# One decoder layer on one core: the turn on which FFN-down takes its fourth pair of half buffers

## The chip, the cores and the metric

The kernel runs on one core of a Trainium2 chip. The metric is the device time of one execution, in microseconds (us); the time of a kernel is the median of several executions. TensorE (PE) multiplies, VectorE (DVE) and ScalarE (ACT) work element by element, GpSimd (POOL) and SyncE (SP) are used here almost only to issue transfers (DMAs) from HBM.

## The reference

One layer of a decoder for 256 tokens of width 2048, all in float32. Cut to the part around the change:

```python
h2 = rms_norm(x, mlp_norm[i])
x = x + jnp.square(jax.nn.relu(h2 @ w_ffn_up[i])) @ w_ffn_down[i]
gate = jax.nn.sigmoid(rms_norm(x, ple_norm[i]) @ w_ple_gate[i])
x = x + gate * (p[i] @ w_ple_proj[i])
return rms_norm(x, final_norm)
```

Ahead of it stand a pooling mixer, an RWKV-7 time mixer and their output product, which the change does not touch. `w_ffn_up` is 2048 x 8192 and `w_ffn_down` 8192 x 2048, 64 MB each; with 256 tokens they are most of the work and most of the bytes.

## The kernel before, in words

**Halves.** Every product is made in TensorE's fast float32 form from two halves of each operand: a high half (what the fast form keeps of the number) and a low half (the rest). A weight block therefore goes through the same steps everywhere: SP loads it raw from HBM (`load_raw`, L158, tiles `raw_*`), ACT copies it in one or two pieces of 128x512 into the high half `wh_*` (L167 in the general helper, L172 in `split_sb`, L1278 in FFN-down), DVE subtracts it from the raw block to get the low half `wl_*` (L168, L173, L1279), and PE multiplies with both.

**Half buffers.** A pair of half buffers (one for `wh`, one for `wl`, 128x1024 each) is free again when PE has made the last product with it. There are three such pairs in the pool `wp` (tags `wh`, `wl`), used in rotation by all stages, and one further pair in the pool `fp` (tags `wh4`, `wl4`) that only FFN-down uses.

**FFN-up.** `ffn_half(hf)` runs twice, each time for one half of the 8192 columns. Its first part makes eight column blocks f (`gemm_wide`, L1112 and L1117; bank `u_w`), each in two halves of four weight blocks `u`. The three pairs in `wp` rotate: weight block k is split into the pair that block k-3 has left. PE needs about the time of four groups of two `wh` and two `wl` products for one weight block. After each half block come the squared ReLU and its halves (`square`: L1356 on ACT, L1357 and L1358 on DVE, tile `r`, then `y`), for seven-product squares also sums of activations (`activation_sums`, tiles `s`, `S`).

**FFN-down.** Its second part is two `down_sweep`s, (hf, pair) for pair 0 and 1, each over 16 square blocks kp of four 512-wide quarters. A square outside `SEVEN` costs eight products of quarters: raw blocks `raw_d_<kp>_0` and `raw_d_<kp>_1`, split into the pairs `<kp>a` and `<kp>b`. A square in `SEVEN` = 1, 3, 4, 6, 8, 9, 11, 13 costs seven (Winograd's form) and needs sums of weight quarters. One of these sums is made by DMA: POOL issues a plain load (L1232) and, when it has landed, a load that adds (L1233) into one of two slots of the tile `ring`. The square's second pair `<kp>b` holds the halves of one raw quarter and, beside it, the halves of this sum from the ring (two ACT copies at L172, two DVE subtractions at L173). From the sum DVE makes `t2` in place (L1313), then two more differences in place in the raw block (L1315); the halves of `t2` go to the tile `wa`, those of the raw block to the pair `<kp>d`, which in three of the four sweeps has buffers of its own. The operands of PE's products stand at L1262 (high by high), L1263 (with the low half of the weight) and L1264 (with the low half of the activation).

**The ring.** `begin_sum` begins the next sum in the list. The first two are begun in FFN-up of the first half, after column blocks 4 and 5 (L1231 is a one-element copy that ties it to `r`); each further one after a seven-product square, into the slot which that square has done with.

**The turn.** `half_tiles` (L1266 to L1271) hands out the pairs of FFN-down. A list `turns`, kept over all four sweeps, counts the calls; on every fourth the pair comes from `fp`, on the other three from `wp`. A sweep takes 32 turns, the last one 37. In a first sweep the order of turns begins 0a, 0b, 1a, 1b, 2a, 2b, 3a, 3b.

**The order.** From FFN-up on, the order of the instructions on each engine is set by the framework's scheduler, which places each instruction by priority as soon as its operands and its buffer are free in its own model of time. The splits of weights and what belongs to them have a raised priority (`tc.high_priority(20000)`). Each engine then runs its list strictly in order: an instruction that waits holds up all that stand behind it on that engine.

Of the kernel before, what the change touches and what calls it, by code (L numbers as in the profile page):

```python
# [40 lines left out]
def trunk(  # L41
# [1176 lines left out]
    turns = []  # L1218
# [20 lines left out]
    def down_sweep(hf, pair, ys, sboxes, hooks=(), between=None):  # L1239
# [26 lines left out]
        def half_tiles(name):  # L1266

            turns.append(name)
            if len(turns) % 4 == 0:
                return [fp.tile([128, 1024], F32R, tag=f"{hl}4", name=f"{hl}_{name}") for hl in ("wh", "wl")]  # L1270
            return [wp.tile([128, 1024], F32R, tag=hl, name=f"{hl}_{name}") for hl in ("wh", "wl")]  # L1271

        def halves_of(src, name, own=False):

            wh, wl = [fp.tile([128, 1024], F32R, tag="graw", bufs=2, name=f"{hl}_{name}") for hl in ("wh", "wl")] if own and hf + pair < 2 else half_tiles(name)
            with tc.high_priority(20000):
                for c in range(2):
                    nc.scalar.activation(wh[:, c * 512 : c * 512 + 512], src[:, c * 512 : c * 512 + 512], AF.Copy)  # L1278
                nc.vector.tensor_tensor(wl, src, wh.bitcast(F32), op=ALU.subtract)  # L1279
            return [(wh[:, c * 512 : c * 512 + 512], wl[:, c * 512 : c * 512 + 512]) for c in range(2)]  # L1280
# [12 lines left out]
        for q, kp in enumerate(visits):  # L1293
# [5 lines left out]
            if kp in seven:  # L1299
                i = SEVEN.index(kp)  # L1300
                st = sboxes[kp][:, i % 2 * 1024 : i % 2 * 1024 + 1024]
                s1, s2_, s3, s4 = ((st[:, c * 128 : c * 128 + 128], st[:, 512 + c * 128 : 640 + c * 128]) for c in range(4))
                p1 = summed(hf, pair, kp)
                t2 = p1
                wa = fp.tile([128, 1024], F32R, tag="junk", bufs=1, name=f"wa{nm}_{kp}")
                w2 = wa[:, 0:512], wa[:, 512:1024]
                w21, w11 = halves_of(rx, f"{nm}_{kp}a")
                wh, wl = half_tiles(f"{nm}_{kp}b")
                w22, w1 = ((wh[:, c : c + 512], wl[:, c : c + 512]) for c in (0, 512))
                with tc.high_priority(20000):  # L1310
                    split_sb(*w22, ry[:, 0:512])
                    split_sb(*w1, p1)
                    nc.vector.tensor_tensor(t2, p1, ry[:, 0:512], op=ALU.subtract)  # L1313
                    t43 = rx.rearrange("p (r n) -> p r n", r=2)
                    nc.vector.tensor_tensor(t43, t43, t2.unsqueeze(1).to_broadcast([128, 2, 512]), op=ALU.subtract)  # L1315
                    split_sb(*w2, t2)
                w4, w3 = halves_of(rx, f"{nm}_{kp}d", True)
                for n, a_, w_ in (("1", a11, w11), ("2", a12, w21), ("3", s4, w22), ("5", s1, w1), ("6", s2_, w2), ("4", a22, w4), ("7", s3, w3)):
                    prod(n, a_, w_)
                begin_sum()  # L1320
            else:
                w21, w11 = halves_of(rx, f"{nm}_{kp}a")
                for n, a_, w_ in (("2", a12, w21), ("4", a22, w21), ("2", a11, w11), ("4", a21, w11)):
                    prod(n, a_, w_)
                w22, w12 = halves_of(ry, f"{nm}_{kp}b")
                for n, a_, w_ in (("3", a12, w22), ("x", a22, w22), ("3", a11, w12), ("x", a21, w12)):
                    prod(n, a_, w_)
# [209 lines left out]
```

## Time and profile before

| | |
|---|---|
| three timed runs | 1179.17, 1180.53, 1183.03 us; median 1180.53 |
| the profiled execution | 1182.91 us, of which 1181.1 us from its first to its last instruction (span) |
| FFN-up, first half | about 378 to 563 us of the span |
| its two sweeps | 563 to 727 us |
| FFN-up and two sweeps, second half | 727 to 1072 us |
| DVE, ACT busy over the span | 877.7 us (74%), 714.1 us (60%) |
| mean granted clock of TensorE | 0.995 of full speed |

All times in the trace are in us from the start of the span. A timeline row gives start, duration, engine, line, operation, tiles, shape, number of instructions merged and, in square brackets, how long the engine had been idle and what released it. PE's instructions overlap: two that start 0.23 us apart last 0.39 us each, so that PE's pace is read from starts and not from durations. A tile's name has its numbers left out: `u_w` is the bank of any column block, and `wh_d_1b` that of square 1 in any of the four sweeps.

### The profile page before, as it was taken

To read this page: it belongs to the slowest core of one execution; us is meant where nothing else is said; L and a number is where in the kernel's file an instruction comes from. 1 tells how busy PE (TensorE), PEld (TensorE's weight loads), DVE (VectorE), ACT (ScalarE), POOL (GpSimd) and SP (SyncE) were. 2 spreads that over 40 slices of the span, in tenths; PEclk is the share of its full clock that TensorE was granted. 3 is DMA by queue.
4 is the path that set the end of the run, shared out by engine and by line. 5 is a ranking of instruction groups with operands and counts; after the bars stand their busy time and mean duration, and the time that the engine had idled before them with its cause. 6 is when DMAs were issued, how large, how long until landed. Compare 5 with 4: busy or idle time off the path is not lost.

```text
span 1181.1 us, 17409 instructions
## 1 busy us (share of the span) xinstructions
PE 1162.8 (98%) x6407; PEld 973.1 (82%) x6407; DVE 877.7 (74%) x1194; ACT 714.1 (60%) x1323; POOL 58.5 (5%) x133
## 2 busy tenths in 40 slices
PE   9999999999999999999999999999999999999997
PEld 8787777788887888878888888888888888888886
DVE  8686996954656676757888988676768988897543
ACT  8777858676545565545665664555556665677543
POOL 2100000000000000000110110000000110000000
PEclk9999999999999999989999999999999999999999
DMA  8454443354454555555687686555555886975511
GB/s 294 154 199 144 142 143 109 119 179 161 175 190 171 179 190 191 198 171 204 202 241 244 200 245 233 194 182 194 186 189 174 248 250 228 316 247 190 198 56 72
DMA packets 67253, 224.42 MB, mean 190 GB/s; under 512 B 7712, under 2 KB 8480, under 8 KB 66784
## 3 DMA queue, kind: packets, MB, share of 16 engines
q1 hardware_dynamic: 60240, 207.38, 50.2%
q0 software_dynamic: 6496, 15.21, 5.7%
q8 instruction: 50, 0.82, 0.3%
q10 hardware_dynamic: 432, 0.73, 0.2%
q14 instruction: 35, 0.29, 0.1%
HBM read 221.19 MB, written 2.10 MB: 189 GB/s over the span
## 4 chain that ended last, share of the span: by engine, by line
PE 93%; DVE 3%; DMA 2%; ACT 2%; issue 1%; POOL 0%; SPq 0%; DVEq 0%; POOLq 0%; ACTq 0%
PE u_w L1112 19%; PE u_w L1117 10%; PE d_b L1262 7%; PE d_b L1264 7%; PE d_b L1263 7%; PE d_w L1262 2%; PE d_w L1264 2%; PE d_w L1263 2%; PE gt_b L238 2%; PE gt_b L241 2%; PE gt_b L242 2%; PE o_b L241 1%; PE o_b L242 1%; PE zv_b L238 1%; PE o_b L238 1%; PE zp_b L238 1%
## 5 line engine op out<-in xcount | busy, mean ns | idle before, releaser
L1112 PE MATMUL u_w<-h,wh_u 128*128 128x512 f32 x1024 | 323.8, 398 | 1.8 <-ACT wh_u L167 1.8
L167 ACT ACTIVATE wh_u<-raw_u 128x512 fp32r<-128x512 f32 x256 | 147.4, 623 | 154.9 <-issue 95.5
L168 DVE TENSOR_TENSOR wl_u<-raw_u,wh_u 128x1024 fp32r<-128x1024 f32 x128 | 156.7, 1224 | 104.6 <-ACT wh_u L167 102.9
L1117 PEld LDWEIGHTS u_w<-h,wl_u 128*128 128x128 f32 x1024 | 193.6, 189 | 47.2 <-DVE wl_u L168 1.5
L1117 PE MATMUL u_w<-h,wl_u 128*128 128x256 f32 x1024 | 202.6, 279 | 0.9 <-DVE wl_u L168 0.9
L1112 PEld LDWEIGHTS u_w<-h,wh_u 128*128 128x128 f32 x1024 | 157.0, 190 | 2.0 <-ACT wh_u L167 2.0
L168 DVE TENSOR_TENSOR wl_gt<-raw_gt,wh_gt 128x1024 fp32r<-128x1024 f32 x24 | 29.4, 1224 | 23.2 <-ACT wh_gt L167 23.1
L172 ACT ACTIVATE wad<-ring 128x512 fp32r<-128x512 f32 x29 | 18.2, 629 | 43.1 <-DVE ring L1313 43.1
L167 ACT ACTIVATE wh_gt<-raw_gt 128x512 fp32r<-128x512 f32 x48 | 28.0, 639 | 23.0 <-PE gt_b L242 14.4
L241 PE MATMUL gt_b<-wh_gt,h 128*128 128x512 f32 x96 | 37.3, 389 | 0.0
L242 PE MATMUL gt_b<-wh_gt,h 128*128 128x512 f32 x96 | 37.3, 389 | 0.0
L1315 DVE TENSOR_TENSOR raw_d<-raw_d,ring 128x1024 f32<-128x1024 f32 x29 | 35.5, 1222 | 0.7
L1232 POOL DMA_DIRECT2D ring<-in_w_ffn_down_dram x29 | 16.5, 570 | 356.8 <-DVE r L1358 190.8
L1233 POOL DMA_DIRECT2D ring<-in_w_ffn_down_dram x29 | 25.4, 876 | 110.4 <-DMA ring<-in_w_ffn_down_dram 110.4
L168 DVE TENSOR_TENSOR wl_o<-raw_o,wh_o 128x1024 fp32r<-128x1024 f32 x16 | 19.6, 1223 | 12.9 <-ACT wh_o L167 11.4
L167 ACT ACTIVATE wh_o<-raw_o 128x512 fp32r<-128x512 f32 x32 | 18.4, 623 | 16.3 <-issue 8.5
L167 ACT ACTIVATE wh_zp<-raw_zp 128x512 fp32r<-128x512 f32 x32 | 18.6, 624 | 15.8 <-PE zp_b L242 7.1
L168 DVE TENSOR_TENSOR wl_zk<-raw_zk,wh_zk 128x1024 fp32r<-128x1024 f32 x16 | 19.4, 1220 | 9.8 <-ACT wh_zk L167 9.8
L241 PE MATMUL zv_b<-wh_zv,hTh 128*128 128x512 f32 x64 | 26.0, 406 | 0.0
L241 PE MATMUL zk_b<-wh_zk,hTh 128*128 128x512 f32 x64 | 25.2, 394 | 0.6 <-ACT wh_zk L167 0.6
L241 PE MATMUL zp_b<-wh_zp,hTh 128*128 128x512 f32 x64 | 25.7, 401 | 0.0
L238 PE MATMUL gt_b<-wl_gt,h 128*128 128x512 f32 x96 | 25.7, 389 | 0.0
(927 smaller groups left out, 3007.2 us busy)
## 6 DMA issues: line engine op xcount, KB each, us to landing
raw_u<-in_w_ffn_up_dram SPq DMA_DIRECT2D x128, 512.0 KB, 3.5
raw_d<-in_w_ffn_down_dram SPq DMA_DIRECT2D x99, 512.0 KB, 4.7
ring<-in_w_ffn_down_dram POOLq DMA_DIRECT2D x58, 256.0 KB, 4.5
raw_gt<-in_w_ple_gate_dram SPq DMA_DIRECT2D x24, 512.0 KB, 3.5
raw_zk<-in_w_in_dram SPq DMA_DIRECT2D x16, 512.0 KB, 3.7
raw_zr<-in_w_in_dram SPq DMA_DIRECT2D x16, 512.0 KB, 3.3
raw_zv<-in_w_in_dram SPq DMA_DIRECT2D x16, 512.0 KB, 3.3
raw_zp<-in_w_in_dram SPq DMA_DIRECT2D x16, 512.0 KB, 3.2
```

The costliest lines, as they stand in the source:

```text
L167: nc.scalar.activation(wh[:, a * 512 : (a + 1) * 512], raw[:, a * 512 : (a + 1) * 512], AF.Copy)
L168: nc.vector.tensor_tensor(wl, raw, wh.bitcast(F32), op=ALU.subtract)
L238: nc.tensor.matmul(banks[tt], ah[:, ts_], halves[a][1], start=False, stop=last)
L241: nc.tensor.matmul(banks[tt], ah[:, ts_], halves[a][0], start=i + a == 0, stop=False)
L242: nc.tensor.matmul(banks[tt], al[:, ts_], halves[a][0], start=False, stop=False)
L1112: nc.tensor.matmul(bank[:, ct, :].rearrange("p (s t) -> p s t", s=2), wh[:, cs[ct]], hl, start=k == 0, stop=False, skip_group_check=True,)
L1117: nc.tensor.matmul(bank[:, ct, 0:T], wl[:, cs[ct]], hl[:, 0, :], start=False, stop=k == 15, skip_group_check=True)
L1233: nc.gpsimd.dma_start(slot(n), w_down[pair, hf * 16 + kp, 0, :, 1, :], accum_op=ALU.add)
L1262: nc.tensor.matmul(banks[n], ah, wh, start=first, stop=False)
L1263: nc.tensor.matmul(banks[n], ah, wl, start=False, stop=False)
L1264: nc.tensor.matmul(banks[n], al, wh, start=False, stop=last)
L1315: nc.vector.tensor_tensor(t43, t43, t2.unsqueeze(1).to_broadcast([128, 2, 512]), op=ALU.subtract)
```

## The change

One number changes: the pair from `fp` is handed out on turns 1, 5, 9 and so on, and no longer on turns 4, 8, 12.

```diff
         def half_tiles(name):
 
             turns.append(name)
-            if len(turns) % 4 == 0:
+            if len(turns) % 4 == 1:
                 return [fp.tile([128, 1024], F32R, tag=f"{hl}4", name=f"{hl}_{name}") for hl in ("wh", "wl")]
             return [wp.tile([128, 1024], F32R, tag=hl, name=f"{hl}_{name}") for hl in ("wh", "wl")]
```

Before, a first sweep's 0a, 0b and 1a take the three pairs that FFN-up leaves, in the order in which it leaves them, and 1b takes the pair in `fp`. Now 0a takes the pair in `fp`, and 0b, 1a and 1b take those that FFN-up leaves. From 2a on every turn again takes the pair of the turn four before it, as it did. Where a second sweep ends and FFN-up follows, the last three turns now hold all three pairs of `wp`; before, it was the last four without the last. No instruction is added or taken away; the scheduler places some of them elsewhere. POOL's list stays as it was.

On ACT, in FFN-up of the first half, just behind the column block that begins the first sum of the ring (`S` is a sum of activations, `wh_u` FFN-up's high halves, `wh_d_1b` those of square 1's second pair):

```order
 L172 ACTIVATE S_4690<-s_4801 128x512
 L167 ACTIVATE wh_u_1_4934<-raw_u_1_4932 128x512 x2
-L172 ACTIVATE wh_d_1b<-ring 128x512
 L167 ACTIVATE wh_u_2_4957<-raw_u_2_4955 128x512 x2
 L1356 ACTIVATE r_0_4902<-u_w_4809 128x512
```

The copy of the ring's sum into the high half of 1b is gone from this place; DVE's list loses its low half (`wl_d_1b<-ring`) at the same place.

On ACT, at the last column block of FFN-up (block 7, its second half, whose weight blocks are `u_0` to `u_3`):

```order
 L172 ACTIVATE y_5018<-r_1_5211 128x512
 L167 ACTIVATE wh_u_0_5327<-raw_u_0_5325 128x512 x2
+L1278 ACTIVATE wh_d_0a<-raw_d_0_0_5429 128x512 x2
 L172 ACTIVATE S_5010<-s_5217 128x512
 L167 ACTIVATE wh_u_1_5350<-raw_u_1_5348 128x512 x2
 L167 ACTIVATE wh_u_2_5373<-raw_u_2_5371 128x512 x2
 L1356 ACTIVATE r_0_5318<-u_w_5225 128x512
-L172 ACTIVATE wh_d_1b<-raw_d_1_1_5469 128x512
 L167 ACTIVATE wh_u_3_5396<-raw_u_3_5394 128x512 x2
-L172 ACTIVATE wad_1_5471<-ring 128x512
-L1278 ACTIVATE wh_d_0a<-raw_d_0_0_5429 128x512 x2
 L172 ACTIVATE y_5224<-r_0_5318 128x512
```

The copies of 0a move ahead of three of FFN-up's last four blocks; the other half of 1b and the halves of `t2` (`wad`) leave FFN-up.

On DVE, where the first sweep begins (`r` is the last squared ReLU of FFN-up):

```order
 L1279 TENSOR_TENSOR wl_d_1a<-raw_d_1_0_5467,wh_d_1a 128x1024
+L173 TENSOR_TENSOR wl_d_1b<-raw_d_1_1_5469,wh_d_1b 128x512
+L173 TENSOR_TENSOR wl_d_1b<-ring,wh_d_1b 128x512
 L1357 TENSOR_TENSOR r_1_5417<-u_w_5324,r_1_5417 128x512
+L1313 TENSOR_TENSOR ring<-ring,raw_d_1_1_5469 128x512
+L1358 SCALAR_TENSOR_TENSOR r_1_5417<-r_1_5417 128x512
 L1315 TENSOR_TENSOR raw_d_1_0_5467<-raw_d_1_0_5467,ring 128x1024
-L1358 SCALAR_TENSOR_TENSOR r_1_5417<-r_1_5417 128x512
+L173 TENSOR_TENSOR wad_1_5471<-ring,wad_1_5471 128x512
 L1279 TENSOR_TENSOR wl_d_2a<-raw_d_2_0_5515,wh_d_2a 128x1024
 L1279 TENSOR_TENSOR wl_d_1d<-raw_d_1_0_5467,wh_d_1d 128x1024
```

Four operations of square 1 (both halves of 1b, `t2` at L1313 and its low half) now stand here, ahead of 1d; the last `y` of FFN-up, which stood between 2b and 3a, now stands behind 3b. The second half's first sweep is changed in the same two ways (its first sum is begun in the second sweep before it, so that its 1b stood early in FFN-up too). The SP list changes only in the order of a few raw loads of the first squares.

## The prediction

> **What bounds the kernel now.** I read the page first. PE is busy 98% of the span, and its granted clock is at the top in every slice but one:
>
> ```profile
> PE 1162.8 (98%) x6407; PEld 973.1 (82%) x6407; DVE 877.7 (74%) x1194; ACT 714.1 (60%) x1323; POOL 58.5 (5%) x133
> PEclk9999999999999999989999999999999999999999
> ```
>
> So a change that removes no product can gain only where PE stands or runs slowly. The 8 is the slice from 502 to 531 us, in FFN-up. The windows around it (PE's busy time and instructions first, granted clock and DMA last):
>
> ```profile
> core 0: us, PE busy (x) PEld busy (x) DVE busy (x) ACT busy (x) POOL busy (x), PEclk, DMA share, GB/s
> 499.00:509.00 10.00, 8.61 (x51) 7.34 (x49) 1.73 (x3) 1.99 (x4) 0.88 (x1) 1.00 0.55 153
> 509.00:519.00 10.00, 8.72 (x33) 7.11 (x34) 7.22 (x8) 5.33 (x11) 0.00 (x0) 0.66 0.44 158
> 519.00:529.00 10.00, 10.00 (x59) 8.71 (x58) 7.64 (x12) 5.99 (x11) 1.73 (x3) 1.00 0.60 206
> ```
>
> Where 59 products start in a normal stretch, 51 and 33 start here; PE idles for a while, and then it runs at 0.66 of its clock. The waits of 495 to 515 us say for whom:
>
> ```profile
> ACT wh_d_1b L172 <- DMA ring<-in_w_ffn_down_dram: 7.9, 1, 7.9
> ...
> PE u_w L1112 <- ACT wh_u L167: 1.8, 1, 1.8
> ...
> PE u_w L1117 <- DVE wl_u L168: 0.9, 1, 0.9
> ```
>
> PE waits for FFN-up's next halves; ACT, which makes them, has stood 7.9 us at a copy that FFN-down will want only some 60 us later: the ring's half of 1b, which could start so early because its buffer, the pair in `fp`, was free. The ring's sum was still on its way. The chain of waits gives its two transfers, the timeline the rest:
>
> ```profile
> 496.31 4.65 DMA ring<-in_w_ffn_down_dram
> ...
> 501.27 6.81 DMA ring<-in_w_ffn_down_dram
> ```
>
> ```profile
> 499.10 1.15 ACT L167 ACTIVATE wh_u<-raw_u 128x512 fp32r<-128x512 f32 x2 [1.11 <-issue]
> ...
> 506.05 0.63 PE L1112 MATMUL u_w<-h,wh_u 128*128 128x512 f32 x2
> 506.75 0.63 PE L1112 MATMUL u_w<-h,wh_u 128*128 128x512 f32 x2
> 508.17 0.63 ACT L172 ACTIVATE wh_d_1b<-ring 128x512 fp32r<-128x512 f32 x1 [7.91 <-DMA ring<-in_w_ffn_down_dram]
> 508.70 1.13 ACT L167 ACTIVATE wh_u<-raw_u 128x512 fp32r<-128x512 f32 x2
> 509.37 0.87 PE L1112 MATMUL u_w<-h,wh_u 128*128 128x512 f32 x2 [1.76 <-ACT wh_u L167]
> 511.74 1.05 PE L1112 MATMUL u_w<-h,wh_u 128*128 128x512 f32 x2
> 513.02 1.05 PE L1112 MATMUL u_w<-h,wh_u 128*128 128x512 f32 x2
> 516.77 0.63 PE L1112 MATMUL u_w<-h,wh_u 128*128 128x512 f32 x2
> ```
>
> PE's groups of two high and two low products start 0.70 us apart (506.05 to 506.75). The next was due at 507.45 and started at 509.37: 1.92 us lost. Up to 516.77 it starts five groups, which at 0.70 take 3.50, so the sixth was due at 507.45 + 3.50 = 510.95 and came at 516.77: **5.82 us lost** in all. After the second pause the groups are 1.28 us apart (511.74 to 513.02), nearly double, until the clock comes back. The lost time is therefore 1.92 and 0.91 us of waiting and 3.0 us of slow clock.
>
> **What the change does, part by part.**
>
> *It removes the early copy.* 1b no longer has a free buffer in FFN-up, so its copy leaves this place on ACT (and its low half on DVE) and comes back at the sweep's start, when that sum has been in the ring for 50 us. Nothing else in ACT's list at this place waits for a DMA of the ring: the next entry is `wh_u`, whose raw block SP loads ahead. Gain: 5.82 us, once. In the second half the same copy sat early too, but there its sum had been begun in the sweep before; PE shows no wait there, so it gains nothing.
>
> [...] The idle rows are 1.8 and 0.9 us, and the clock fell. [...]
>
> *It puts 0a early into FFN-up.* ACT now copies 0a (two pieces) behind the first of the last four weight blocks. What is queued behind it on ACT is FFN-up's next `wh_u`, for which PE waits. The raw block of 0a must have landed by then:
>
> ```profile
> raw_d<-in_w_ffn_down_dram SPq DMA_DIRECT2D x1, 512.0 KB, 3.5
> ```
>
> ```profile
> 543.57 0.33 SPq L158 DMA_DIRECT2D raw_d<-in_w_ffn_down_dram  x1
> ```
>
> ```profile
> 546.76 1.15 ACT L167 ACTIVATE wh_u<-raw_u 128x512 fp32r<-128x512 f32 x2 [1.16 <-issue]
> ```
>
> It lands at 543.57 + 3.5 = 547.1; ACT is through with the block ahead at 547.9. So there is no wait, with 0.8 us to spare, and if the load is late ACT has the slack of FFN-up besides: in the stall above the copy would have started at 501.9 (one block, 4 x 0.70, after 499.10), started at 508.70, and PE was 1.92 us late, so 4.9 us are free. Cost: none. ACT's 1.15 us and DVE's 1.22 us for 0a only change places. SP: raw loads of the first squares are issued in another order, each still behind a buffer that comes free no later than before; no cost.
>
> *It delays 1b at the start of both first sweeps.* 1b, `t2` and its halves now queue there. Rows of before, DVE, ACT, PE and POOL:
>
> ```profile
> 569.27 1.22 DVE L1279 TENSOR_TENSOR wl_d_1d<-raw_d,wh_d_1d 128x1024 fp32r<-128x1024 f32 x1
> ...
> 571.54 0.68 DVE L173 TENSOR_TENSOR y<-r,y 128x512 fp32r<-128x512 f32 x1
> ...
> 577.83 1.23 DVE L1279 TENSOR_TENSOR wl_d_3d<-raw_d,wh_d_3d 128x1024 fp32r<-128x1024 f32 x1 [0.68 <-ACT wh_d_3d L1278]
> ...
> 586.05 1.22 DVE L1279 TENSOR_TENSOR wl_d_4d<-raw_d,wh_d_4d 128x1024 fp32r<-128x1024 f32 x1
> ```
>
> ```profile
> 563.48 1.15 ACT L1278 ACTIVATE wh_d_1a<-raw_d 128x512 fp32r<-128x512 f32 x2 [1.64 <-issue]
> ...
> 579.89 0.62 ACT L172 ACTIVATE wh_d_4b<-ring 128x512 fp32r<-128x512 f32 x1
> ```
>
> ```profile
> 572.53 0.39 PE L1263 MATMUL d_b<-wl_d_1d,y 128*128 128x512 f32 x1
> ...
> 587.50 0.39 PE L1263 MATMUL d_b<-wl_d_4d,y 128*128 128x512 f32 x1
> ```
>
> 1a had waited for FFN-up's last pair until 563.48; now 1b gets that pair, then. From its first ACT copy on (0.63, till 564.1) DVE has, up to 1d: six small ones of 0.68 (1b twice, L1357, L1313, L1358, `wad`) and two large ones of 1.22 (L1315, 2a), 6.5 us by whole durations, so 1d starts at 570.6 and is ready at 571.8 where PE takes it at 572.53. That is 0.7 us to spare, or more, since the rows overlap a little. DVE is then at most 1.4 us behind the row of before (570.6 against 569.27). The `y` that moved behind 3b is passed on, and the gap of 0.68 before 3d is used up, which leaves 0 to 0.7 us at square 4. There the rows are tightest: `wl_d_4d` ends at 587.27, used at 587.50, 0.23 spare. Cost: 0 to 0.5 us a sweep; the low end is nearer, as the overlaps take most of the 1.4.
>
> *It delays a sum in the ring.* The third sum goes into the slot that square 1 has done with, and square 4 uses it. POOL's load for it now waits for `wad` of square 1, which ends, by the same count without 2a, at 564.1 + 6 x 0.68 + 1.22 = 569.4 at the latest:
>
> ```profile
> 568.17 0.56 POOL L1232 DMA_DIRECT2D ring<-in_w_ffn_down_dram  x1 [40.65 <-DVE raw_d L1315]
> ```
>
> so it is about 1.2 us later. The 29 loads, and the 29 adding loads after them, landed in (minimum, median, maximum):
>
> ```profile
> L1232 POOL DMA_DIRECT2D ring<-in_w_ffn_down_dram x29: 561/565/718, 496.3 to 1018.6; - x29
> ...
> DMA to landing us min/median/max: 2.9/3.7/6.1
> ```
>
> ```profile
> L1233 POOL DMA_DIRECT2D ring<-in_w_ffn_down_dram x29: 863/875/899, 501.3 to 1025.1; - x29
> ...
> DMA to landing us min/median/max: 3.8/6.6/9.0
> ```
>
> With the medians and the 0.31 us between the two (500.96 to 501.27): 569.4 + 3.7 + 0.3 + 6.6 = 580.0, against ACT's copy at 579.89. It is on time to a tenth; cost 0.1 us a sweep, none at the minima, more at the maxima (the second rival).
>
> *Back into FFN-up, and at the end.* After the second sweep FFN-up's second block must now wait for 15a's pair and the third for 15b's, a turn later each:
>
> ```profile
> 724.20 1.15 ACT L167 ACTIVATE wh_u<-raw_u 128x512 fp32r<-128x512 f32 x2 [2.41 <-PE d_b L1264]
> ```
>
> ```profile
> 726.67 0.61 PE L1112 MATMUL u_w<-h,wh_u 128*128 128x512 f32 x2
> ```
>
> 15a's pair comes free at 724.2, so the second block is split by 724.2 + 1.15 + 1.22 = 726.6, and PE wants it at 726.67 + 2.8 = 729.5; the third is 2.5 us later in both. DVE's updates of the residual stand among these, cover of 2.9 us. Cost none. In the last stages a few transposes and copies change places; no row prices that, so between a gain and a loss of the smaller wait above, 0.9 us, and I take 0.
>
> **Sum:** -5.82 + 2 x 0.1 = -5.6 us. The profiled execution took 1182.91 (a span of 1181.1 and 1.8 around it), and would take 1177.3. It lies 2.4 above the median of the timed runs, 1180.53; from that, **1174.9 us**.
>
> **Rivals.** *The stall is smaller in the timed runs.* From the ring's landing at 508.08 to PE's start went 1.29 us, and PE was due at 507.45; a sum that landed before 506.16, 4.9 us after its issue, would cost nothing. Of 29, the quickest took 3.8, the median 6.6. For it speaks that the timed runs spread by 3.9 us and that their median lies 2.4 under the profiled one: if that is all stall, 3.4 us are left to gain, 1177.1, and with no stall 1180.5. Against it: 6.8 us is an ordinary time among the 29. Chance 0.14. [...]
>
> *The clock is not lost in the timed runs,* only the waiting, 1.92 + 0.91 = 2.8: 1180.5 - 2.8 + 0.2 = 1177.9. Only the one profiled pause speaks, and it speaks against. Chance 0.05.
>
> *The wait moves into the sweeps, and it is slower.* At the maxima the third sum lands at 569.4 + 6.1 + 0.3 + 9.0 = 584.8, 4.9 late; halfway between median and maximum 2.4 late, of which 0.23 are spare: PE then waits 2.2 us at 4d and loses 3.0 of clock behind it, 5.2 in each of two sweeps, 10.4: 1180.5 - 5.8 + 10.4 = 1185.1. It decides from a landing 0.7 us after 579.89 on (each sweep then loses 0.5 + clock). For: spare is a tenth. Against: both loads must be late, in both sweeps. Chance 0.07.
>
> *The change does not do what it says:* the stall stays, because ACT meets another late transfer in FFN-up (0a's raw block would have to take over 9 us, its rows say 3.5). 1180.5; chance 0.04.
>
> **The numbers.** The forecast has 0.70. Its own range is half the spread of the runs of before, 1.9, to either side: 1173.0 to 1176.8; the 0 to 1.0 us of waits in the sweeps lie inside it. To hold eight in ten it must take in the 1177.1 and 1177.9 of the first rivals and part of the way to 1180.5: 1173.0 to 1179.3. About 0.3%, 3.5 us, can be told from no change, so faster begins under 1177.0. Faster 0.70; same, with three rivals, 0.23; slower 0.07.
>
> **What would show it.** Right: no `wh_d_1b` on ACT before 555 us, a PE clock of 1.00 at 500 to 520, groups 0.70 apart throughout, `wh_d_0a` copied behind the first of the last four blocks without a wait, and a span of about 1175.5. Wrong: a wait of PE at `wl_d_4d` or at 1d in a first sweep, ACT idle before `wh_d_4b` for the ring, a PE gap behind the second sweep, or a stall of before that the timed runs never had.

## The result, and the profile after

In the same session the changed kernel took **1177.88 us** (median of 22 runs, 1176.85 to 1179.6) and the kernel before 1182.13 us (22 runs, 1176.46 to 1184.43). The ratio of the two sets of runs is 0.9971, 95% interval 0.9962 to 0.9979: 0.29% faster, a hair under the 0.3% that the prediction called faster. (The two medians alone are 4.25 us apart, 0.36%.) The forecast of 1174.9 was 3.0 us too low; 1177.88 lies above its own range (to 1176.8) and within the wider one, where the first rival stands (1177.1 to 1180.5). The base of the forecast, 1180.53, was a median of three runs; that of the 22 is 1.6 us higher.

The profiled execution, in contrast, came out as forecast: 1177.39 us with a span of 1175.5 (forecast 1177.3 and about 1175.5). That it comes so close is in part luck: both profiled executions kept their clock at 37 us (1.00 from 36 to 44 us), where others lose 1.7 us (below). PE's row and the clock's row on the page of the changed kernel:

```profile
PE 1160.3 (99%) x6407; PEld 971.5 (83%) x6407; DVE 877.4 (75%) x1194; ACT 713.8 (61%) x1323; POOL 57.2 (5%) x133
PEclk9999999999999999999999999999999999999999
```

The 8 in the clock's row is gone. The windows around that place, in the changed kernel (PE's busy time and starts first, granted clock ninth):

```profile
499.00:509.00 10.00, 10.00 (x60) 8.76 (x59) 6.25 (x8) 5.62 (x10) 0.88 (x1) 1.00 0.79 223
509.00:519.00 10.00, 10.00 (x59) 8.71 (x58) 6.86 (x10) 4.83 (x9) 0.87 (x2) 1.00 0.55 197
```

60 and 59 products start where 51 and 33 did. What the ring's tile did from 495 to 515 us in the changed kernel (its instructions, who waited for the tile, and issue to landing of the two transfers):

```profile
L1233 POOL DMA_DIRECT2D ring<-in_w_ffn_down_dram x1: 877/877/877, 500.6 to 500.6; - x1
...
who waited for it (us, times):
  POOL ring L1233: 3.6, 1
  POOL ring L1232: 0.3, 1
...
DMA to landing us min/median/max: 4.0/5.8/7.7
```

The adding load took 7.7 us, longer than in the profile of before (6.81), and landed at 508.3, past the 506.16 up to which the prediction had a landing cost nothing. But only POOL itself waits for the ring: ACT has no copy standing here any more.

The rows that the prediction named, all from the timeline of the changed kernel. On ACT, the two pieces of 0a in FFN-up, with no wait ahead of them:

```profile
541.99 1.14 ACT L1278 ACTIVATE wh_d_0a<-raw_d 128x512 fp32r<-128x512 f32 x2
```

On DVE, the low halves of 1d and 4d in the first sweep:

```profile
564.16 1.22 DVE L1279 TENSOR_TENSOR wl_d_1d<-raw_d,wh_d_1d 128x1024 fp32r<-128x1024 f32 x1
...
580.21 1.22 DVE L1279 TENSOR_TENSOR wl_d_4d<-raw_d,wh_d_4d 128x1024 fp32r<-128x1024 f32 x1
```

On PE, the first products with them:

```profile
566.71 0.39 PE L1263 MATMUL d_b<-wl_d_1d,y 128*128 128x512 f32 x1
...
581.67 0.39 PE L1263 MATMUL d_b<-wl_d_4d,y 128*128 128x512 f32 x1
```

On POOL, the two transfers of the third sum:

```profile
563.40 0.56 POOL L1232 DMA_DIRECT2D ring<-in_w_ffn_down_dram  x1 [41.75 <-DVE wad L173]
566.65 0.89 POOL L1233 DMA_DIRECT2D ring<-in_w_ffn_down_dram  x1 [2.69 <-DMA ring<-in_w_ffn_down_dram]
```

On ACT, the second block of FFN-up's return, behind 15a's pair:

```profile
718.37 1.15 ACT L167 ACTIVATE wh_u<-raw_u 128x512 fp32r<-128x512 f32 x2 [2.74 <-PE d_b L1264]
```

1d is ready at 565.38 and used at 566.71, 1.3 us to spare (forecast 0.7 or more); 4d is ready at 581.43 and used at 581.67, 0.24 (before 0.23). PE loses nothing from 380 to 1040 us of this profile.

So the one profiled pair confirms the sum to a tenth, and the medians do not. The runs of before say why. Over four sessions there are 133 runs of that kernel (its unchanged copy below among them). They fall into two groups, with only four runs between 1180.1 and 1181.2: 75 runs under 1180.5 with a mean of 1178.2, and 58 above with a mean of 1183.2. The changed kernel's 34 runs have a mean of 1178.3, and none is above 1179.8. The change takes away the upper group and leaves the lower where it was.

### The profile page after: what moved, and what is told of

It reads as the page before. It is cut to its first block, busy times and chain, and to the rows that moved or that the text cites. A ratio compares the mean times of both kernels' runs of the same rounds, so it can differ in the third digit from the quotient of the medians.

```text
span 1175.5 us, 17403 instructions
## 1 busy us (share of the span) xinstructions
PE 1160.3 (99%) x6407; PEld 971.5 (83%) x6407; DVE 877.4 (75%) x1194; ACT 713.8 (61%) x1323; POOL 57.2 (5%) x133
## 4 chain that ended last, share of the span: by engine, by line
PE 94%; DVE 2%; ACT 2%; DMA 1%; issue 0%; SPq 0%; DVEq 0%; ACTq 0%
PE u_w L1112 20%; PE u_w L1117 10%; PE d_b L1262 7%; PE d_b L1263 7%; PE d_b L1264 7%; PE d_w L1262 2%; PE d_w L1263 2%; PE d_w L1264 2%; PE gt_b L241 2%; PE gt_b L238 2%; PE gt_b L242 2%; PE o_b L241 1%; PE o_b L242 1%; PE zv_b L238 1%; PE o_b L238 1%; PE zv_b L241 1%
## 5 line engine op out<-in xcount | busy, mean ns | idle before, releaser
L167 ACT ACTIVATE wh_zk<-raw_zk 128x512 fp32r<-128x512 f32 x32 | 18.4, 622 | 12.3 <-PE zv_b L242 4.0
```

The costliest lines, as they stand in the source:

```text
L167: nc.scalar.activation(wh[:, a * 512 : (a + 1) * 512], raw[:, a * 512 : (a + 1) * 512], AF.Copy)
```

## The experiments

Two theories were set against each other. **Theory V:** the stall is worth 5 to 6 us, but comes only in those executions in which the ring's first sum lands late; elsewhere the change costs nothing. **Rival G:** the stall is lost every time, and the changed kernel gives some 2 us back somewhere. Later expectations add theories (R, P and O) on the smaller groups within the stall-free runs. Times are medians, and each ratio is to the kernel before as it ran in the same session. That kernel took 1179.26 us (35 runs) beside its own unchanged copy, the rotation moved in the second half alone, and one load less and one more for its first sum. It took 1178.59 us (29 runs) beside the rotation moved in the first half alone and the three edits of sums on the changed kernel, and 1180.43 us (35 runs) beside the last four.

### The kernel before once more

No edit.

> The kernel before, unchanged, for its single executions. Theory V (the stall varies): the ring's first sum lands earlier in part of the executions, so that their times spread over 1177 to 1184 us, and the time goes with the mean granted clock: about 0.998 where it is near 1178, 0.995 where it is near 1183; the stall in the new profile is smaller or larger than 5.8 us, by the landing of the adding load, with 4.9 us after its issue as the point under which there is none. Rival G (given back): the stall is the same 5.8 us in every execution, so the clock is 0.995 in nearly all of them and their spread has nothing to do with it; the changed kernel pays some 2 us elsewhere.

Measured: 1181.13 us, 12 runs; ratio 1.0006 (0.9984 to 1.0028). Five runs lie at 1176.69 to 1177.42, one at 1179.9, six at 1182.35 to 1184.68. The profile fell on an execution without the stall (span 1175.4). Its ring tile at 495 to 515 us, and the window:

```profile
L1233 POOL DMA_DIRECT2D ring<-in_w_ffn_down_dram x1: 877/877/877, 500.5 to 500.5; - x1
L172 ACT ACTIVATE wh_d_1b<-ring x1: 633/633/633, 505.0 to 505.0; 128x512 fp32r<-128x512 f32 x1
...
  ACT wh_d_1b L172: 4.6, 1
...
DMA to landing us min/median/max: 3.7/4.1/4.4
```

```profile
509.00:519.00 10.00, 10.00 (x60) 8.71 (x59) 8.93 (x12) 6.27 (x12) 0.87 (x2) 1.00 0.82 266
```

Same code, same place: ACT waits 4.6 us instead of 7.9, because the sum landed at 504.9 and not at 508.1. Of these 3.2 us, 0.8 come from the plain load ahead, which landed sooner, so that the adding load was issued at 500.48 instead of 501.27; 2.4 come from the adding load, which took 4.4 us instead of 6.8. The prediction's break-even, a landing at 506.16, lies between the two. PE stays busy at a clock of 1.00. The mean granted clock of the runs goes with their groups, as theory V expected: 0.998 or 0.999 in the five, 0.995 to 0.997 in the six.

### The rotation moved in the second half alone

```diff
-            if len(turns) % 4 == 0:
+            if len(turns) % 4 == (0 if hf == 0 else 1):
```

> The turn is changed in the second half alone; the first half is as before. Theory V: no gain and no cost, ratio to before 0.999 to 1.001, and the stall near 500 to 517 us is still there, between 0 and 6 us. Rival G, if what is given back lies in the sweeps' starts, the return into FFN-up or the end: half of it or more shows here, so 1 to 2 us slower than before, with a wait of PE after 885 us.

Measured: 1179.12 us (1176.87 to 1184.34, 12 runs), ratio 0.9993 (0.9971 to 1.0015). Two groups as before, 7 runs under 1180.6 and 5 above. The profile has the stall in the first half: the adding load took 7.9 us, and the window and the wait show it.

```profile
509.00:519.00 10.00, 8.11 (x36) 6.72 (x37) 7.40 (x8) 6.29 (x13) 0.00 (x0) 0.83 0.49 153
```

```profile
ACT wh_d_1b L172 <- DMA ring<-in_w_ffn_down_dram: 8.3, 1, 8.3
...
PE u_w L1112 <- ACT wh_u L167: 2.2, 1, 2.2
```

From 727 us on PE waits for nothing in this profile. The second half's rotation shows neither gain nor cost, and the stall of this profile is in the first half.

### The rotation moved in the first half alone

```diff
-            if len(turns) % 4 == 0:
+            if len(turns) % 4 == (1 if hf == 0 else 0):
```

> The rotation moved in the first half alone; the second half keeps that of before. Theory V (the kernel before loses about 5.8 us in those executions in which the ring's first sum lands late; the change takes that away in the first half and costs nothing elsewhere): the whole gain is there, so the time is that of the changed kernel, 1177.9 within 1, PE 10.00 busy of 10 at 499 to 519 us at a clock of 1.00. Where FFN-up comes back, at about 716 to 727 us, the early copy of the second half is now placed ahead of the first weight block; if its sum lands as late as in the trace of before, PE could lose up to 1 us there. Rival G (the stall was lost in every execution and the changed kernel gives some 2 us back elsewhere): if the second half's rotation is what gives back, 1176; if the first half's, 1177.9 too.

Measured: 1177.26 us (1176.38 to 1179.42, 12 runs), ratio 0.9989 (0.9978 to 1.0000), with only 5 of the 29 runs beside it in the upper group. No run is in that group here, which 12 runs against 5 in 29 would not show by themselves. But the profile has no wait of PE from 380 to 1072 us and none of ACT for a transfer of the ring, while with the second half alone 5 of 12 runs have the stall. The effect is in the first half.

### One load less for the first sum, on the kernel before

```diff
-            nc.gpsimd.dma_start(slot(n), ..., accum_op=ALU.add)
+            if n: nc.gpsimd.dma_start(slot(n), ..., accum_op=ALU.add)
```

> The kernel before with its turns, but the first sum of the ring is one plain load without the adding load; the second weight quarter is left out of that one sum. The early copy stays and moves one weight block ahead. By the rows of before its load lands 4.65 us after 496.3, ACT waits about 3.5 us for it, inside the 4.9 us that FFN-up has free: no wait of PE and no slow clock. Theory V: about as the changed kernel, 1178, ratio to before 0.996 to 0.998. Rival G: the whole stall without the price of the new turns, 1176.3, ratio 0.995.

Measured: 1177.95 us (1176.75 to 1178.9, 12 runs), ratio 0.9981 (0.9964 to 0.9999): the changed kernel's time, with the old rotation, and no run above 1178.9, where 15 of the 35 beside it are in the upper group. The scheduler put the copy one weight block earlier, and ACT still waits there, for less than the break-even:

```profile
ACT wh_d_1b L172 <- DMA ring<-in_w_ffn_down_dram: 2.6, 1, 2.6
```

So the early copy itself is harmless; what costs is a sum that lands late for it. Rival G, by which 1176.3 was due here, falls.

### One load more for the first sum, on the kernel before

```diff
-            nc.gpsimd.dma_start(slot(n), ..., accum_op=ALU.add)
+            for _ in range(1 if n else 2): nc.gpsimd.dma_start(slot(n), ..., accum_op=ALU.add)
```

> The kernel before with its turns, but the first sum has two adding loads in place of one, so that the weight quarter is added twice. The early copy stays, one weight block later, and its sum lands about 6.6 us later: ACT waits about 12 us, PE about 6 us in place of 1.9, and the clock falls as before. Theory V: the stall is there in every execution, 8 to 12 us, so 1186 to 1190, ratio 1.003 to 1.007. Rival G: the same size, so this run tells only whether PE's loss follows the sum's landing; no change at all would speak against the early copy as the cause.

Measured: 1185.57 us (1180.36 to 1187.5, 12 runs), ratio 1.0039 (1.0018 to 1.0060). The lowest run stands alone at 1180.36 and the other eleven are at 1184.6 and above: the lower group is gone. The expected 1186 to 1190 was a little too high; ACT waited 9.6 us and not about 12. The window and the waits:

```profile
509.00:519.00 10.00, 5.12 (x18) 3.69 (x17) 5.89 (x7) 4.86 (x9) 0.00 (x0) 0.74 0.34 77
```

```profile
ACT wh_d_1b L172 <- DMA ring<-in_w_ffn_down_dram: 9.6, 1, 9.6
...
PE u_w L1112 <- ACT wh_u L167: 3.9, 1, 3.9
```

The loss follows the landing of this one sum, up as well as down.

### One load more for the first sum, on the changed kernel

```diff
+            for _ in range(1 if n else 2): nc.gpsimd.dma_start(slot(n), ..., accum_op=ALU.add)
```

(in place of the adding load, as above, with the new rotation)

> The changed kernel with a third transfer for the first sum: the adding load is issued twice, so one quarter counts twice in it and it lands some 4 us later. On the kernel before, the same edit cost 3.4 us of the median and put the stall into the profiled execution. Theory V: here nobody waits for that sum in FFN-up, so 1177.9 within 1, no idle time of PE at 490 to 520 us and a clock of 1.00. Rival (the changed kernel still meets the late sum somewhere, only later): slower than the changed kernel by 2 to 6 us.

Measured: 1177.88 us (1177.38 to 1180.54, 12 runs), ratio 0.9998 (0.9987 to 1.0008). From 495 to 520 us nobody but POOL waits for the ring:

```profile
L1233 POOL DMA_DIRECT2D ring<-in_w_ffn_down_dram x2: 861/870/880, 501.9 to 508.6; - x2
...
who waited for it (us, times):
  POOL ring L1233: 12.8, 3
  POOL ring L1232: 0.6, 2
```

A delay that the old rotation pays with its whole lower group costs nothing here: the change makes the kernel independent of this landing, as far as this delay tests it. (The 3.4 us in the expectation are counted from the 1182.13 of another session; beside its own 1179.26 the edit cost the kernel before 6.3 us of the median.)

### One load more for the third sum, on the changed kernel

```diff
+            for _ in range(2 if n == 2 else 1): nc.gpsimd.dma_start(slot(n), ..., accum_op=ALU.add)
```

> The changed kernel with the adding load of the third sum (square 4 of the first sweep, first half) issued twice, so one quarter counts twice in it. In the trace of the changed kernel this sum lands at 573.37 and is copied at 574.07, and the square's last operand is ready 0.24 us before PE takes it, so 0.9 us later is free. The extra load takes 4 to 7 us. If the prediction's slower rival had its mechanism right (the wait moves into the sweep): ACT waits 3.5 to 6.5 us at the copy into 4b, PE waits 2.5 to 5.5 us at square 4 and loses about 3 us of clock behind it, 1183 to 1187. If other slack covers a late sum there: below 1180.

Measured: 1185.06 us (1182.8 to 1186.76, 6 runs), ratio 1.0056 (1.0041 to 1.0071). Waits of 570 to 595 us, and the window:

```profile
ACT wh_d_4b L172 <- DMA ring<-in_w_ffn_down_dram: 4.5, 1, 4.5
...
PE d_b L1263 <- DVE wl_d_4d L1279: 1.3, 1, 1.3
PE d_w L1263 <- DVE wad L173: 1.2, 1, 1.2
...
PE d_w L1262 <- ACT wad L172: 1.0, 1, 1.0
```

```profile
580.00:590.00 10.00, 6.47 (x22) 4.39 (x22) 9.08 (x11) 6.46 (x12) 1.43 (x2) 0.89 0.71 212
```

PE loses 6.0 us between 583 and 592 (this profile, with a span of 1183.0, loses 1.7 more at 39 us, of which below). The prediction's slower rival had the place right. Its price is near (5.2 us for a sum 2.4 us late, against 6.0 here with ACT 4.5 us behind), but not its parts: PE's waits are 3.5 us and the slow clock costs 1.7, where it had 2.2 and 3.0. What it lacked is the late sum. In the changed kernel that sum lands 0.7 us ahead of its copy (573.37 against 574.07).

### No adding loads, on the changed kernel

```diff
-            nc.gpsimd.dma_start(slot(n), ..., accum_op=ALU.add)
+            pass
```

> The changed kernel with no adding loads at all: every sum of the ring is one plain load, the other quarter is left out of all 29 sums; the order on ACT, DVE and SP is the same. Of the changed kernel's 22 runs 13 lie at 1176.85 to 1178.0 and 9 at 1178.7 to 1179.6. Theory R (in the upper group a sum of the ring lands late in a sweep, where 0.9 us is free, the price of the delay that the prediction put at 0.1 us a sweep): here every sum lands about 7 us earlier, the upper group is gone, and the median is 1177.3. Theory O (the upper group has nothing to do with the ring): both groups stay, median 1177.9 within 0.5, runs above 1178.5 still among them.

Measured: 1178.59 us (1176.87 to 1179.72, 12 runs), ratio 0.9999 (0.9989 to 1.0009). Six of 12 runs are above 1178.45, so the smaller split of the stall-free runs, 1177 against 1179, does not come from the ring; theory R falls. The profile fell on an execution of the upper part (1179.41) and shows where it is: PE's first product after a pause at 37 us, in the stage before the time mixer, and below it the window around it.

```profile
38.22 0.41 PE L464 MATMUL wagT<-ident,wagS 128*128 128x128 f32 x2 [1.59 <-POOL wband L132]
```

```profile
36.00:44.00 8.00, 6.41 (x26) 5.02 (x26) 5.05 (x16) 5.38 (x10) 4.23 (x15) 0.79 0.34 108
```

26 products start where 36 do in the changed kernel's own profile, whose pause is 0.95 us and whose clock there is 1.00. The lower clock alone costs PE 1.7 us in this window (0.21 x 8). The profiles with one load more for the first and for the third sum of the changed kernel show the same clock of 0.79 there, behind pauses of 1.73 and 1.16 us. Nothing that the change touches lies before 380 us.

### The pause at 37 us, shortened, lengthened and shortened otherwise

Three edits of the changed kernel, and the changed kernel beside them. `steps` sets how many products of `zk` PE makes between the sums of squares and the transposes `wagT`. One more:

```diff
-        steps(1)
+        steps(2)
```

> The changed kernel, and at about 37 us of the span, long before FFN, one more product of zk ahead of the transposes wagT. In eleven profiles PE's pause there is 0.95 to 1.40 us with no loss of clock, and 1.59 and 1.73 us in the two that show a granted clock of 0.79 at 36 to 44 us and spans of 1177.7 and 1176.9. Theory P (the upper group of all kernels' runs, 1178.5 to 1179.6, is this pause: past about 1.5 us the clock falls for some 3 us, at a price of 1.7): the pause is 0.23 shorter, so most upper runs go and the median is 1177.2 within 0.4. Theory O (the upper group has another cause): as many runs above 1178.5 as without the edit, 4 in 10.

Measured: 1177.97 us (1177.33 to 1180.18, 12 runs), 4 runs above 1178.45; ratio 0.9987 (0.9973 to 1.0002). The profile's pause is 0.67 us with a clock of 1.00. The expectation had the profiles wrong: of the ten by then, the kernel before pauses 1.66 us without a loss of clock, and the one with the longer third sum loses it after 1.16.

One less:

```diff
-        steps(1)
+        steps(0)
```

> The opposite edit: no product of zk between the sums and the transposes wagT, so PE's pause at 37 us is 0.23 longer, 1.2 to 1.95 us. Theory P: more runs lose their clock there; over 6 in 10 above 1178.5, median 1178.7 within 0.6, and a profile with a pause over 1.5 us shows a clock under 0.9 at 36 to 44 us. Theory O: 4 in 10 above 1178.5, median 1177.9.

Measured: 1178.22 us (1177.17 to 1181.3, 12 runs), 4 runs above 1178.45 and not over 6 in 10, two of them at 1181.07 and 1181.3, which no run here explains; ratio 0.9983 (0.9968 to 0.9998). The profile (1179.45) does have a long pause and the lower clock:

```profile
37.73 0.41 PE L464 MATMUL wagT<-ident,wagS 128*128 128x128 f32 x2 [1.71 <-ACT wagS L459]
```

```profile
36.00:44.00 8.00, 6.29 (x25) 5.10 (x25) 4.64 (x16) 5.20 (x11) 4.15 (x15) 0.79 0.33 95
```

One more, and the square root and reciprocal of the normalisation at a raised priority:

```diff
-        steps(1)
+        steps(2)
...
-    head_norm()
+    with tc.high_priority(20000): head_norm()
```

> The changed kernel with the product moved as in the first of these runs, and besides the normalisation's ACT and DVE steps at a raised priority: one of the two copies of wh_zr, which wait for a transfer, then stands behind the square root instead of ahead of it, up to 0.5 us earlier. Theory P: the pause is under 1.2 us in every execution, no run above 1178.5, median 1177.0 within 0.4, so under the changed kernel's. Theory O: 4 in 10 above 1178.5.

Measured: 1177.46 us (1176.91 to 1178.86, 12 runs), one run above 1178.45; ratio 0.9979 (0.9966 to 0.9993). Theory P's "no run above 1178.5" and its 1177.0 within 0.4 are both missed by a little. On ACT the square root now stands between the two copies of `wh_zr`; in the changed kernel it stands behind both:

```profile
36.27 0.26 ACT L450 ACTIVATE rs_n<-sbank,eps_n 128x2 f32<-128x2 f32 x1 [0.39 <-PE sbank L441]
36.43 0.62 ACT L167 ACTIVATE wh_zr<-raw_zr 128x512 fp32r<-128x512 f32 x1
```

The changed kernel beside them, without an edit.

> The changed kernel unchanged, for its two groups of times on this chip. Both theories: a lower group at 1176.8 to 1178.2 and an upper at 1178.5 to 1179.6, 4 of 10 runs in the upper, median 1177.9 within 0.5; no run above 1181, where before has its stall.

Measured: 1178.85 us (1176.79 to 1179.76, 12 runs), 7 runs above 1178.45, none above 1181, and a median 0.45 us over the expected range; ratio 0.9982 (0.9967 to 0.9997). In the profile PE loses 0.65 us at square 9 of the first sweep, the only such loss in the profiles of unaltered sums under the new rotation:

```profile
ACT wh_d_6b L172 <- DMA ring<-in_w_ffn_down_dram: 2.6, 1, 2.6
...
PE d_b L1263 <- DVE wl_d_9d L1279: 0.4, 1, 0.4
```

The sum of square 6 took 7.7 us from the issue of its adding load (576.50 to 584.17) and held up ACT, and DVE behind it by 1.8 us; the slack of the squares between ate most of it.

What follows for the smaller split: of the ten profiles with neither the stall nor the longer third sum, the three over 1178.45 us (1178.65, 1179.41 and 1179.45) lose their clock behind this pause, and none of those under it does. The version with both edits has 1 run of 12 in the upper part against 16 of 34 of the changed kernel, and is the quickest of those run with the changed kernel beside it: a mean of 1177.6 against 1178.6. That the shorter pause does this is suggested, not shown. Its profiled pause, 0.78 us, is no shorter than the 0.67 of the first edit, which left 4 of 12; one product more or less (0.23 us) alone did not move the counts as theory P expected; and a threshold at 1.5 us is refuted by the 1.16 and the 1.66. The pause is where the clock goes; its length does not decide when.

## Why the prediction was wrong, point by point

**The sum was set against the wrong base.** The step that failed is the gain, "Gain: 5.82 us, once", subtracted from the median as if every execution held it. By their times, 58 of 133 executions of before have the stall (from 5 of 29 to 15 of 22 by session), and it is worth 1183.2 - 1178.2 = 5.0 us where it is. 0.44 x 5.0 = 2.2 us is the mean gain, and 1180.35 - 1178.3 = 2.1 is what the pooled means show. In the session of the result 15 of 22 runs had it, 0.68 x 5.0 = 3.4; the means there are 1181.6 and 1178.1. The base of 1180.53, the median of three runs, lay between the two groups: with 5.8 us taken off, the forecast came out under every run of either kernel. The count is an estimate, since only a profile shows the stall itself and three runs of variants that no longer have it still lie at 1180.5 to 1181.3.

**The case that came was the first rival,** "the stall is smaller in the timed runs", given 0.14, in a sharper form: not smaller, but absent in about half of them. The prediction noted the evidence and passed it by. Three runs spread over 3.9 us, two thirds of the stall's size; the profiled execution lay 2.4 over the median; the adding load took 3.8 to 9.0 us over its 29 instances; and a break-even of 4.9 us lies inside that spread. The runs show that this one load varies as much between executions, 4.0 to 7.9 us at the same place (4.4 us in the copy of before without the stall, 6.8 and 7.9 us in two profiles with it), so a wait for it is a chance, not an amount.

**The mechanism was right in the parts that the runs tested.** The stall is the first half's early copy behind a late sum (one load less removes it, one more puts it into nearly every run), and the second half gains nothing. 0a in FFN-up, 1b at the sweep's start and the return to FFN-up cost nothing: the changed kernel's mean is within 0.1 us of the lower group of before. The break-even stood, as the time at which the sum lands (506.16) rather than as the length of one load: landings at 504.9 cost nothing, those at 508.1 and 508.5 did.

**The lost clock was real.** Of the windows with a stall, the clock is 0.66, 0.83 and 0.74 in the three profiles of 509 to 519 us. The rival by which only the waiting was lost falls. The price varies, though: the first sweep begins at 557.77 in the copy without the stall, at 563.46 in the profile of before and at 562.99 in that of the second half alone, where the clock was slow for half as long. So 5.82 us was one size of several, and 5.0 is the mean.

**The delayed sums in the sweeps** were priced at 0.1 us a sweep. Six profiles of the new rotation with its sums unaltered in the sweeps show nothing over 0.1 us, one shows 0.65. The third sum lands 0.7 us before its copy. The slower rival is not seen in 34 runs; that it would cost 5 to 6 us a sweep is (6.0).

**What stays open:** why the same adding load takes some 4 us in one execution and 7 in the next. The rows suggest an answer that no run tested. SP issues a raw load of FFN-up shortly behind it, here in before and then in its copy without the stall:

```profile
501.54 0.33 SPq L158 DMA_DIRECT2D raw_u<-in_w_ffn_up_dram  x1
```

```profile
501.66 0.33 SPq L158 DMA_DIRECT2D raw_u<-in_w_ffn_up_dram  x1
```

That is 0.3 us behind the adding load of 501.27 and 1.2 us behind that of 500.48. Twelve profiles have an adding load for the first sum. In the seven with the raw load 0.3 to 1.0 us behind, the adding load takes 6.8 to 7.9 us and the two land within 0.3 us of each other. In the three with 1.1 to 1.2 us (1.14 and more) it takes 4.0 to 4.4. At 1.08 us there is one of each, 4.2 and 6.4. That the two slow each other when they are issued close together is what these rows suggest; no run moved one against the other.

## What to carry to other kernels

When the profiled execution and the median of the runs differ by more than the usual scatter, ask first whether the stall that you see is in every run, and multiply its price by its share before you subtract it. A wait for a transfer that holds up the instructions behind it, as ACT's 7.9 us at the ring's copy held up FFN-up's next `wh_u`, is a chance whose price begins at the slack behind it (ACT's waits of 2.6 and 4.6 us there cost PE nothing, those of 7.9 to 9.6 us did): write down the break-even landing and compare it with the whole spread of that transfer, not with its median. Moving the waiting instruction away from the urgent ones may gain little in the median and still be worth it, since it takes the long executions away.

## What the runs showed of the hardware

**A pause of 1.16 us came with a loss of clock and one of 1.66 us without: the length does not settle it.** PE's pause at 37 us was 0.67, 0.78, 0.85, 0.95, 1.07, 1.27, 1.37, 1.40, 1.44 and 1.66 us in ten profiles with a granted clock of 1.00 at 36 to 44 us, and 1.16, 1.59, 1.71 and 1.73 us in four with 0.79. The two that cross, first the kernel before, pause and window:

```profile
37.54 0.41 PE L464 MATMUL wagT<-ident,wagS 128*128 128x128 f32 x2 [1.66 <-POOL wband L130]
```

```profile
36.00:44.00 8.00, 6.46 (x32) 5.42 (x33) 6.02 (x17) 5.71 (x12) 3.73 (x14) 1.00 0.37 121
```

Then the changed kernel with the longer third sum:

```profile
37.47 0.41 PE L464 MATMUL wagT<-ident,wagS 128*128 128x128 f32 x2 [1.16 <-POOL wband L131]
```

```profile
36.00:44.00 8.00, 6.84 (x26) 5.28 (x26) 5.12 (x16) 5.18 (x10) 4.10 (x15) 0.79 0.32 107
```

**The clock's losses in these profiles are 1.7 us each, or twice that.** In the stall of before the granted clock is half, 0.50 in each window of 1 us from 510 to 516 us, as in this one:

```profile
513.00:514.00 1.00, 1.00 (x5) 0.81 (x4) 1.00 (x2) 1.00 (x3) 0.00 (x0) 0.50 0.69 279
```

In windows of 0.05 us the clock falls there at 509.83 us and rises at 516.66: 6.83 us at 0.50, 3.4 us lost, as the 0.66 over 10 us has it. All four of the windows at 37 us have 0.79: 0.21 x 8 = 1.7 us lost, which at the same half speed would be 3.4 us of slow running, an estimate. The pace of PE behind the pause of 1.16 us agrees: its products start 0.43 us apart from 38.88 to 41.44 us, against 0.23 before the pause (33.65 to 34.56). In the other stalls, 0.83 over 10 us is 1.7 again (the second half's kernel); with one load more it is 0.74 and then 0.92 in the next 10 us, 3.4.

**What PE did around the pause does not settle it either.** These are two stretches of that estimated length, 3.4 us; each holds the whole of its pause, the first that of 1.66 us in the kernel before, the second that of 1.16 us in the kernel with the longer third sum:

```profile
35.36:38.78 3.42, 1.76 (x12) 1.31 (x12) 1.37 (x6) 2.65 (x6) 2.83 (x11) 1.00 0.51 176
```

```profile
34.90:38.31 3.41, 2.25 (x18) 1.84 (x17) 1.67 (x4) 2.26 (x6) 2.07 (x8) 1.00 0.52 183
```

PE is busy for 1.76 us in the first, and the clock stays; it is busy for 2.25 us in the second, and the clock is lost behind it. So neither a longer pause nor less work of PE in these stretches goes with the loss, and what decides stays open.
